# Delta rule, phase one: the keys' chain over more steps, gates' projections and the inversion spread anew

## The chip, the cores and the metric

One core of a Trainium2 chip runs the whole decoder trunk in one launch. The metric is the device time of one execution in microseconds (us); smaller is better. Engines named here: TensorE (PE in the rows, with PEld for its weight loads and "matmul" for what it runs), VectorE (DVE), ScalarE (ACT), GpSimd (POOL) and SyncE (SP), whose queue issues all the DMAs spoken of here.

## What is computed

Four residual layers of 1024 tokens x 1024 features: a gated convolution, forgetting attention, the gated delta rule, and sliding-window attention. The change lies in the third, the delta rule (8 heads of 128, chunks of the sequence). Its heart, cut from the reference (`k_beta` is k times beta):

```python
    L = jnp.where(strict, jnp.einsum('bhnid,bhnjd->bhnij', k_beta, k) * decay, 0.0)
    T = lax.linalg.triangular_solve(eye + L, jnp.broadcast_to(eye, L.shape), left_side=True, lower=True, unit_diagonal=True)
    u = T @ v_beta
    w = T @ (k_beta * jnp.exp(g_cum)[..., None])
    ...
    def step(state, xs):
        qd, kd, u_c, w_c, qk_c, gl = xs
        v_new = u_c - w_c @ state
        o = qd @ state + qk_c @ v_new
        state = state * jnp.exp(gl)[..., None, None] + jnp.einsum('bhck,bhcv->bhkv', kd, v_new)
        return state, o
    ...
    return (o * jax.nn.silu(z)) @ w_out
```

k comes from a projection, a causal convolution of four taps, SiLU and a normalisation; z is a projection too, and silu(z) is what the kernel calls a gate.

## The kernel before

Everything is laid out as 128 features x 512 tokens, two halves h of the sequence. Projections run in split float32: each chunk of 128 input features is three 512-column matmuls (high x high, high x low, low x high; L159 to L161), eight chunks for one output tile, and `proj_steps` yields after each. Weights are loaded raw and split in two parts, a ScalarE cast (hi) and a GpSimd subtraction (lo; `split_w`, L142 and L143; for gates `zsplit`, L1675 and L1676, tiles cv and QK).

Phase one of `layer_gdn` prepares the keys of 8 heads x 2 halves, numbered n = 0 to 15, and computes the gates beside them. `step(n)` for n = 1 to 17 strings pieces of generators together: `cur` is `keys(n)` (from step 16 on it is gates, then the later `fill`), `stage(m)` advances the keys started in step m by one yield, `zfill` advances the gates by one chunk, `dec` and `decs` the decay tile E, `g.advance(0, r)` the inversion by r yields. TensorE runs in the order in which this is written all through the phase, ScalarE and GpSimd do in steps 1 to 15; the order of VectorE and of SyncE is chosen by the framework's planner.

One key's pieces by yield, which the steps below name by number:

- 1 to 8: chunks of its projection (TensorE); 9: cb and cu from PSUM (ScalarE, L1297 and L1305), three conv instructions (VectorE, L1307)
- 10: tanh (ScalarE, L1313) and the last product, which gives kT (VectorE, L1314); 11: kT is stored by DMA
- 12: four transposes of kT (TensorE, L1322), four squares with sums (ScalarE, L1330), rk (VectorE, L1361), a power (GpSimd, L1362), kq (VectorE, L1364)
- 13: kd, four scalings (ScalarE, L1369), its store, kg and E x rk (GpSimd, L1371 and L1374), the store of E
- 14: a small transpose of kq (TensorE, L1379), its copy to a row (ScalarE, L1381) and the row's store gbr; 15: the load that spreads that row, br (L1385)
- 16: br x E (GpSimd, L1387); 17: four matmuls pa of kT with itself (TensorE, L1392), LT = pa x br (VectorE, L1394), its store gLT; 18: the load of the diagonal blocks into U (L1412, `blocks`)

In the kernel before, key n takes yields 1 to 10 in step n; 11 and 12 after five chunks of step n+1, 13 after the rest of its chunks, 14 at its end; 15 at the start of step n+2, 16 in the middle, 17 at its end; 18 at the start of step n+3.

`solve` inverts the 32 x 32 diagonal blocks of heads 0 to 3 (b = 0), row by row: for row i a product over i x i elements (split in two from row 23 on, L1428) and a reduction (L1431), all on VectorE, 71 yields and a last one that stores T twice (L1433, L1435, with a copy between). It needs U of keys 0 to 7. Steps 10 to 15 advance it by 6, 3 and 3 yields each. After step 15 `loads(0, 0)` brings T back as the tiles T1 and TT (L1461, L1459); `merge` (L1477 and on) uses them from the eleventh piece of step 17's `fill` on, and then the scan over chunks begins. Tiles have fixed buffers: E (TT) 3, kT 3, LT 3 (shared with a gate's raw weights), br (qT) 2, PSUM of pa 2.

Of the kernel before, what the change touches and what calls it, by code (L numbers as in the profile page):

```python
# [1186 lines left out]
class Gdn:  # L1187
# [226 lines left out]
    def solve(self, b, U):  # L1414
        p, nc = self.p, self.nc
        T = p.tile([P, 32, 32], F32, name="sT")
        nc.vector.memset(T, 0.0)
        nc.vector.memset(T.rearrange("p a b -> p (a b)")[:, 0:1024:33], 1.0)
        pr = p.tile([P, HT], F32, name="sp")
        for i in range(1, 32):  # L1420
            step = HT // i
            for n0 in range(0, i, step):
                n1 = min(i, n0 + step)
                n = n1 - n0

                m = i - n0
                v = pr[:, :n * m].rearrange("p (n j) -> p n j", j=m)
                nc.vector.tensor_tensor(v, T[:, n0:i, n0:n1].rearrange("p j n -> p n j"),  # L1428
                                        U[:, n0:i, i].unsqueeze(1).broadcast_to([P, n, m]), op=ALU.mult)
                yield  # L1430
                nc.vector.tensor_reduce(T[:, i, n0:n1], v, axis=AX.X, op=ALU.add, negate=True)  # L1431
            yield
        nc.sync.dma_start(out=self.T_d[b][0], in_=T)  # L1433
        nc.vector.tensor_copy(U, T.rearrange("p i n -> p n i"))
        nc.sync.dma_start(out=self.T_d[b][1], in_=U)  # L1435
        yield
# [211 lines left out]

FILL = 1300
HOPS = 13  # L1650
ZF = 5
LAG = 5

MORE = (25, 0, -25)
# [2 lines left out]
def layer_gdn(k, out):  # L1657
    with k.tc.tile_pool(name="gd", bufs=1) as p:
        g = Gdn(k, p)
# [21 lines left out]
        def gate(c, h):  # L1681
            load = h and c < 7
            if load:
                raws.append(zraw(c + 1, 1))
            for i, u in enumerate(k.gate2_steps(zs[c], c, h)):
                if i == 0 and not h and 0 < c < 7:
                    raws.append(zraw(c + 1, 0))
                if load and i % 4 == 3:
                    zsplit(c + 1, raws.pop(0))
                yield u  # L1690
# [11 lines left out]
        def take(it, n=1):  # L1702
            for _ in range(n):
                next(it, None)
# [3 lines left out]
        def stage(n, count=1):  # L1708
            take(stages.get(n, none), count)

        with k.tc.manual_schedule(engines={E_.PE}):
            other = k.gate2_steps(zs[0], 0, 1)
            for _ in range(8):
                take(half, 1)
                take(other, 1)
            take(half, 1)
            take(other, 1)
            gts = g.gates()
            take(gts, 17)
            zfill = itertools.chain(gate(1, 1), *(gate(c, h) for c in range(2, 8) for h in range(NH)))  # L1720
            g.wload(1, 0)
            fill = itertools.chain(*(g.prepare(i // 2, i % 2) for i in range(16)),
                                   itertools.islice(out, 6), g.values(), out)
            stages[0] = g.keys(0, 0, g.w[1])
            stage(0, 5)
            take(gts)
            stage(0, 4)
            take(zfill, ZF + 5)
            take(gts)
            take(zfill, 3)  # L1730
            take(gts)
            stage(0)
            late = g.decay(0, 0)
            take(late)

            def step(n):
                hd, h = n // 2, n % 2
                dec = decs.pop(0)
                if n < 16:
                    cur = stages[n] = g.keys(hd, h, g.w[1])  # L1740
                else:
                    cur = zfill if n == 16 else fill
                stage(n - 2)
                stage(n - 3)
                if n < 15 and h:
                    wraw = kraw.pop(0)
                    g.w[1] = [k.split_w(r, P) for r in wraw]
                if n > 1:
                    take(dec)
                if 10 <= n < 16:  # L1750
                    g.advance(0, 6)
                take(cur, 5)
                stage(n - 1, 2)
                take(cur, 4 if n < 16 else 3)
                if n == 1:
                    take(late, 2)
                    take(dec)
                stage(n - 1)
                stage(n - 2)
                if n < 14 and not h:  # L1760
                    kraw.append([k.raw_wk(g.w_in[j * 512:(j + 1) * 512, 1024 + (hd + 1) * P:1024 + (hd + 2) * P], P) for j in range(2)])
                if 10 <= n < 16:
                    g.advance(0, 3)
                take(zfill if n < 17 else fill, ZF)
                take(dec)
                if n < 16:
                    take(cur)
                decs.append(g.decay((n + 1) // 2, (n + 1) % 2) if n < 15 else none)
                take(decs[0])
                stage(n - 2)  # L1770
                stage(n - 1)
                if 10 <= n < 16:
                    g.advance(0, 3)
                if n == 14:
                    g.wload(0, 0)
                if n == 15:
                    g.wload(2, 0)

            decs = [g.decay(0, 1)]
            take(decs[0])  # L1780
            kraw = [[k.raw_wk(g.w_in[j * 512:(j + 1) * 512, 1024 + P:1024 + 2 * P], P) for j in range(2)]]
            with k.tc.manual_schedule(engines={E_.Activation, E_.Pool}):
                for n in range(1, 16):
                    step(n)
            g.ahead.append(g.loads(0, 0))
            for j in range(2):
                g.kd_load(j)
            step(16)
            step(17)
            stage(15)  # L1790
            take(zfill, 30)
            g.advance(1, 24)
            done = 0
            for i in range(16):
                while len(g.prep.get((i // 2, i % 2), ())) < 6:
                    next(fill)
                for j, extra in enumerate(g.scan(i // 2, i % 2)):
                    if i == 14 and j < 7:
                        k.split_y(j, 0)
                    quota = FILL // HOPS + (extra or 0)  # L1800
                    while done < quota:
                        c = next(fill)
                        done += c
                        if c == 0:

                            assert i == 15 and j > 3
                    done -= quota
            for _ in range(3):
                next(out)
            run(g.tail())  # L1810
            with k.tc.issue_after(k.mark.ins):
                for c in range(7):
                    k.split_y(c, 1)
# [72 lines left out]
```

## Time and profile before

| | |
|---|---|
| time, median of 3 runs | 2153.03 us (2152.46 to 2154.45) |
| profiled execution, its own time | 2149.09 us |
| its span, first to last instruction | 2147.4 us |
| TensorE busy | 2078.8 us, 97% |
| VectorE, ScalarE, GpSimd busy | 1323.6 us, 992.1 us, 836.8 us |
| mean granted TensorE clock | 0.992 |
| chain that ended last | TensorE 74%, VectorE 13%, ScalarE 4%, DMA 4% |

The profiled execution is one run: its span and 1.7 us around it are its time, and it lies 3.9 us under the median of the three. Times in the rows are microseconds from the span's start. An engine's busy share is an average over the whole program; what matters for the change is the stretch of phase one, from about 1080 to 1290 us. The ends of matmuls are modelled and overlap, so distances between their starts are used.

### The profile page before, as it was taken

To read this page: it belongs to the slowest core of one execution; us is meant where nothing else is said; L and a number is where in the kernel's file an instruction comes from. 1 tells how busy PE (TensorE), PEld (TensorE's weight loads), DVE (VectorE), ACT (ScalarE), POOL (GpSimd) and SP (SyncE) were. 2 spreads that over 40 slices of the span, in tenths; PEclk is the share of its full clock that TensorE was granted. 3 is DMA by queue.
4 is the path that set the end of the run, shared out by engine and by line. 5 is a ranking of instruction groups with operands and counts; after the bars stand their busy time and mean duration, and the time that the engine had idled before them with its cause. 6 is when DMAs were issued, how large, how long until landed. Compare 5 with 4: busy or idle time off the path is not lost.

```text
span 2147.4 us, 33391 instructions
## 1 busy us (share of the span) xinstructions
PE 2078.8 (97%) x11717; PEld 1748.3 (81%) x11717; DVE 1323.6 (62%) x2748; ACT 992.1 (46%) x2483; POOL 836.8 (39%) x721
## 2 busy tenths in 40 slices
PE   7999999999999999999999789999999999999998
PEld 5887888788898989888688677878888888878888
DVE  7657655544535355475455967775565568888874
ACT  6333334433433233454366443434443446666764
POOL 2244544731221221236356552322324545445630
PEclk9999999999999999999999999999999999999999
DMA  7122213741222321236256553342325521121134
GB/s 237 50 69 84 64 59 119 224 95 41 47 38 44 40 51 31 58 95 187 75 159 195 157 171 96 87 122 78 102 80 164 168 66 49 46 54 50 45 89 148
DMA packets 288366, 205.70 MB, mean 96 GB/s; under 512 B 41381, under 2 KB 245574, under 8 KB 288198
## 3 DMA queue, kind: packets, MB, share of 16 engines
q1 hardware_dynamic: 288198, 203.56, 33.9%
q8 instruction: 93, 1.52, 0.3%
q14 instruction: 75, 0.61, 0.1%
HBM read 154.87 MB, written 43.38 MB: 92 GB/s over the span
## 4 chain that ended last, share of the span: by engine, by line
PE 74%; DVE 13%; ACT 4%; DMA 4%; issue 3%; POOL 1%; SPq 0%; ACTq 0%; POOLq 0%; DVEq 0%
PE ps_pj L159 15%; PE ps_pj L160 15%; PE ps_pj L161 15%; PE ps_sc L248 2%; PE ps_sc L250 2%; PE ps_sc L249 2%; PE ps_pj L248 1%; PE ps_pj L249 1%; PE ps_pj L250 1%; PE ps_tr L835 1%; DVE sp L1428 1%; DVE cu L1307 1%; DVE lg L1153 1%; PE ps_pj L743 1%; PE ps_pj L745 1%
## 5 line engine op out<-in xcount | busy, mean ns | idle before, releaser
L159 PE MATMUL ps_pj<-hhi,whi 128*128 128x512 f32 (+1 forms) x1712 | 698.8, 409 | 3.5 <-ACT hhi L411 1.4
L160 PE MATMUL ps_pj<-hlo,whi 128*128 128x512 f32 (+1 forms) x1712 | 669.2, 391 | 7.2 <-DVE hlo L416 3.9
L161 PE MATMUL ps_pj<-hhi,wlo 128*128 128x512 f32 (+1 forms) x1712 | 669.0, 391 | 0.0
L143 POOL TENSOR_TENSOR wlo<-wraw,whi 128x512 fp32r<-128x512 f32 x296 | 404.4, 1373 | 615.9 <-ACT whi L142 584.9
L161 PEld LDWEIGHTS ps_pj<-hhi,wlo 128*128 128x128 f32 x1712 | 321.8, 188 | 68.9
L160 PEld LDWEIGHTS ps_pj<-hlo,whi 128*128 128x128 f32 x1712 | 323.3, 189 | 61.6 <-DVE hlo L416 5.1
L159 PEld LDWEIGHTS ps_pj<-hhi,whi 128*128 128x128 f32 x1712 | 323.1, 189 | 59.7 <-issue 2.5
L142 ACT CAST whi<-wraw 128x512 fp32r<-128x512 f32 x304 | 185.9, 617 | 312.1 <-PE ps_pj L160 172.7
L1307 DVE SCALAR_TENSOR_TENSOR cu<-cb,taps,cu 128x512 f32<-128x512 f32 x144 | 135.7, 942 | 12.3 <-ACT cu L1305 10.5
L1159 POOL TENSOR_TENSOR lg<-lg,st 128x512 f32<-128x512 f32 (+1 forms) x64 | 63.7, 996 | 122.7 <-DVE st L1158 117.3
L888 ACT ACTIVATE lg<-lg,mx 128x512 f32<-128x512 f32 (+2 forms) x96 | 58.7, 613 | 64.0 <-DVE mx L883 63.6
L1156 ACT ACTIVATE lg<-lg,st 128x257 f32<-128x257 f32 (+1 forms) x128 | 63.1, 494 | 49.2 <-DVE st L1153 49.0
L840 ACT CAST phi<-ps_tr 128x512 fp32r<-128x512 f32 (+1 forms) x80 | 40.6, 544 | 94.3 <-PE ps_tr L835 94.2
L461 DVE TENSOR_TENSOR y<-ps_pj,xr 128x512 f32<-128x512 f32 x56 | 38.5, 687 | 64.0 <-PE ps_pj L161 57.5
L841 DVE TENSOR_TENSOR plo<-ps_tr,phi 128x512 fp32r<-128x512 f32 (+1 forms) x80 | 49.5, 633 | 42.5 <-ACT phi L840 42.5
L469 DVE TENSOR_TENSOR acc<-acc,hf 128x512 f32<-128x512 f32 x49 | 48.5, 990 | 41.2 <-ACT hf L468 41.2
L143 POOL TENSOR_TENSOR wlo<-wr,whi 128x512 fp32r<-128x512 f32 x36 | 48.0, 1333 | 59.0 <-ACT whi L142 54.7
L1428 DVE TENSOR_TENSOR sp<-sT,sU 128x504 f32<-128x504 f32 (+18 forms) x80 | 57.0, 713 | 6.3 <-DMA sU<-gLT 5.1
L1153 DVE CUSTOM_DVE_ANT_0 lg<-ps_sc,band,sk 128x256 f32<-128x256 f32 (+1 forms) x128 | 55.0, 464 | 5.0 <-PE ps_sc L1148 3.4
L291 DVE SCALAR_TENSOR_TENSOR y<-y,ps_pj 128x512 f32<-128x512 f32 x48 | 32.7, 681 | 38.6 <-ACT y L290 38.6
L743 PE MATMUL ps_pj<-whi,hhi 128*128 128x256 f32 x192 | 54.8, 285 | 0.0
L744 PE MATMUL ps_pj<-wlo,hhi 128*128 128x256 f32 x192 | 54.6, 285 | 0.0
(448 smaller groups left out, 4613.5 us busy)
## 6 DMA issues: line engine op xcount, KB each, us to landing
xd<-y SPq DMA_DIRECT2D x64, 256.0 KB, 3.4
wraw<-in_fox_w_in_dram SPq DMA_DIRECT2D x60, 256.0 KB, 4.2
xr<-xd SPq DMA_DIRECT2D x56, 256.0 KB, 2.8
wraw<-in_gdn_w_in_dram SPq DMA_DIRECT2D x52, 256.0 KB, 3.7
wraw<-in_conv_w_in_dram SPq DMA_DIRECT2D x40, 256.0 KB, 3.0
wraw<-in_swa_w_in_dram SPq DMA_DIRECT2D x40, 256.0 KB, 2.9
wraw<-in_conv_w_out_dram SPq DMA_DIRECT2D x32, 256.0 KB, 4.9
wraw<-in_fox_w_out_dram SPq DMA_DIRECT2D x32, 256.0 KB, 2.8
```

The lines of the kernel that those rows point to most:

```text
L142: nc.scalar.copy(hi[:, :, :cols], raw[:, :, :cols])
L143: (eng or nc.gpsimd).tensor_tensor(lo[:, :, :cols], raw[:, :, :cols], hi[:, :, :cols].bitcast(F32), op=ALU.subtract)
L159: nc.tensor.matmul(o, hi, xhi, start=(c == 0), stop=False)
L160: nc.tensor.matmul(o, hi, xlo, start=False, stop=False)
L161: nc.tensor.matmul(o, lo, xhi, start=False, stop=(c == NC_ - 1))
L248: nc.tensor.matmul(ps, whi[:, c, :], xhi, start=start and c == 0, stop=False, skip_group_check=True)
L249: nc.tensor.matmul(ps, whi[:, c, :], xlo, start=False, stop=False, skip_group_check=True)
L250: nc.tensor.matmul(ps, wlo[:, c, :], xhi, start=False, stop=stop and c == 3, skip_group_check=True)
L743: nc.tensor.matmul(ps, xhi, whi, start=(c == 0), stop=False)
L1153: nc.vector.tensor_tensor_reduce(lg[:, u, :n], ps[:, u, :n], band[:, 2 * P - n:], 1.0, sk[:, hd:hd + 1], ALU.add, ALU.min, st[:, 0, u:u + 1])
L1307: eng.scalar_tensor_tensor(u, cb[:, j:j + HT], tap(j), u, op0=ALU.mult, op1=ALU.add)
L1428: nc.vector.tensor_tensor(v, T[:, n0:i, n0:n1].rearrange("p j n -> p n j"), U[:, n0:i, i].unsqueeze(1).broadcast_to([P, n, m]), op=ALU.mult)
```

## The change

Three numbers and the order inside `step` change; no instruction is added or taken away.

- A step takes 3 gate chunks (ZF) in steps 1 to 9 and 8 (ZL, four in the middle and four later) in steps 10 to 16, where it took 5 in each.
- The keys' pieces come later: 11 and 12 after all chunks of step n+1 and behind its conv, 13 at its end; 14 after two chunks of step n+2, 15 after five, 16 at its end; 17 at the start of step n+3, 18 in the middle.
- The inversion is advanced by the numbers of ROWS, three pieces in each of steps 10 to 15 (12, 12, 12, 10, 10 and 9 yields) and what is left in step 16; the first piece stands after five chunks. Step 16 is therefore issued ahead of `loads(0, 0)` and the first loads of kd.

```diff
--- before.py
+++ after.py
@@ -1648,7 +1648,10 @@
 
 FILL = 1300
 HOPS = 13
-ZF = 5
+
+ZF, ZL = 3, 8
+
+ROWS = {10: (4, 4, 4), 11: (4, 4, 4), 12: (4, 4, 4), 13: (4, 3, 3), 14: (4, 3, 3), 15: (3, 3, 3), 16: (99,)}
 LAG = 5
 
 MORE = (25, 0, -25)
@@ -1725,7 +1728,7 @@
             stage(0, 5)
             take(gts)
             stage(0, 4)
-            take(zfill, ZF + 5)
+            take(zfill, 10)
             take(gts)
             take(zfill, 3)
             take(gts)
@@ -1740,37 +1743,39 @@
                     cur = stages[n] = g.keys(hd, h, g.w[1])
                 else:
                     cur = zfill if n == 16 else fill
-                stage(n - 2)
+                rows = list(ROWS.get(n, ()))
+                solve = lambda: rows and g.advance(0, rows.pop(0))
                 stage(n - 3)
                 if n < 15 and h:
                     wraw = kraw.pop(0)
                     g.w[1] = [k.split_w(r, P) for r in wraw]
                 if n > 1:
                     take(dec)
-                if 10 <= n < 16:
-                    g.advance(0, 6)
-                take(cur, 5)
-                stage(n - 1, 2)
+                take(cur, 2)
+                stage(n - 2)
+                take(cur, 3)
+                stage(n - 2)
+                stage(n - 3)
+                solve()
+                if n in ROWS:
+                    take(zfill, ZL // 2)
                 take(cur, 4 if n < 16 else 3)
                 if n == 1:
                     take(late, 2)
                     take(dec)
-                stage(n - 1)
-                stage(n - 2)
+                stage(n - 1, 2)
                 if n < 14 and not h:
                     kraw.append([k.raw_wk(g.w_in[j * 512:(j + 1) * 512, 1024 + (hd + 1) * P:1024 + (hd + 2) * P], P) for j in range(2)])
-                if 10 <= n < 16:
-                    g.advance(0, 3)
-                take(zfill if n < 17 else fill, ZF)
+                solve()
+                take(zfill if n < 17 else fill, ZF if n < 10 else ZL - ZL // 2 if n < 17 else 5)
                 take(dec)
                 if n < 16:
                     take(cur)
+                stage(n - 2)
+                stage(n - 1)
                 decs.append(g.decay((n + 1) // 2, (n + 1) % 2) if n < 15 else none)
                 take(decs[0])
-                stage(n - 2)
-                stage(n - 1)
-                if 10 <= n < 16:
-                    g.advance(0, 3)
+                solve()
                 if n == 14:
                     g.wload(0, 0)
                 if n == 15:
@@ -1782,12 +1787,12 @@
             with k.tc.manual_schedule(engines={E_.Activation, E_.Pool}):
                 for n in range(1, 16):
                     step(n)
+            step(16)
             g.ahead.append(g.loads(0, 0))
             for j in range(2):
                 g.kd_load(j)
-            step(16)
             step(17)
-            stage(15)
+            stage(15, 2)
             take(zfill, 30)
             g.advance(1, 24)
             done = 0
```

## Rows read from the trace of the kernel before

**Rows 1.** The page: busy time, share of the span, instructions.

```profile
PE 2078.8 (97%) x11717; PEld 1748.3 (81%) x11717; DVE 1323.6 (62%) x2748; ACT 992.1 (46%) x2483; POOL 836.8 (39%) x721
```

**Rows 2.** Windows: length, busy time (instructions) by engine, clock, DMA share, GB/s.

```profile
1090.25:1173.89 83.64, 83.64 (x417) 69.50 (x417) 47.50 (x65) 55.20 (x179) 56.30 (x61) 1.00 0.66 197
1173.89:1260.96 87.07, 68.78 (x313) 55.16 (x312) 77.08 (x132) 43.32 (x137) 54.71 (x50) 0.94 0.57 161
```

**Rows 3.** What TensorE waited for, 1173.89 to 1260.96 (us, times, longest).

```profile
PE ps_tr L1322 <- DVE kT L1314: 15.0, 5, 5.2
PE ps_pj L161 <- POOL QK L1676: 2.7, 1, 2.7
PE ps_pj L159 <- ACT cv L1675: 0.6, 1, 0.6
```

**Rows 4.** Timeline of TensorE, step 8 and the first merge (start, length, instruction).

```profile
1152.99 0.60 PE L1322 MATMUL ps_tr<-ident,kT 128*128 128x128 f32 x4
...
1155.51 0.39 PE L159 MATMUL ps_pj<-hhi,cv 128*128 128x512 f32 x1
...
1159.00 1.05 PE L1392 MATMUL ps_sc<-kT 128*128 128x128 f32 x8
1159.89 0.27 PE L1379 MATMUL ps_ov<-ident,kq 128*4 128x128 f32 x1
...
1274.91 0.59 PE L1477 MATMUL ps_pj<-T,LT 32*32 32x32 f32 x16
```

**Rows 5.** Groups of VectorE's instructions, 1178 to 1251 (busy us, mean ns, idle before).

```profile
L1428 DVE TENSOR_TENSOR sp<-sT,sU 128x1 f32<-128x1 f32 (+29 forms) x40 | 32.3, 807 | 5.9 <-DMA sU<-gLT 5.1
L1431 DVE TENSOR_REDUCE sT<-sp 128x1 f32<-128x1 f32 (+30 forms) x40 | 15.5, 387 | 0.8
L1307 DVE SCALAR_TENSOR_TENSOR cu<-cb,taps,cu 128x512 f32<-128x512 f32 x15 | 14.9, 995 | 0.0
L1314 DVE SCALAR_TENSOR_TENSOR kT<-kT,cu 128x512 f32<-128x512 f32 x5 | 4.5, 895 | 0.0
```

**Rows 6.** Timeline of VectorE and GpSimd in the inversion.

```profile
1203.43 0.80 DVE L1428 TENSOR_TENSOR sp<-sT,sU 128x361 f32<-128x361 f32 x1
...
1216.76 2.78 POOL L143 TENSOR_TENSOR wlo<-wraw,whi 128x512 fp32r<-128x512 f32 x2 [1.96 <-ACT whi L142]
...
1217.06 1.24 DVE L1428 TENSOR_TENSOR sp<-sT,sU 128x1 f32<-128x1 f32 x1
```

**Rows 7.** Timeline of ScalarE, step 8: squares (first, last), cb, cu.

```profile
1153.68 0.28 ACT L1330 ACTIVATE jk<-ps_tr 128x128 f32<-128x128 f32 x1 [3.34 <-PE ps_tr L1322]
...
1155.06 0.19 ACT L1330 ACTIVATION_READ_ACCUMULATOR jk<-ps_tr 128x1 f32 x1
1155.71 0.59 ACT L1297 COPY cb<-ps_pj 128x512 f32<-128x512 f32 x1 [0.45 <-PE ps_pj L161]
1156.19 0.69 ACT L1305 ACTIVATE cu<-ps_pj,taps 128x512 f32<-128x512 f32 x1
```

**Rows 8.** Timeline of VectorE, step 8: rk and kq.

```profile
1155.29 0.24 DVE L1361 TENSOR_SCALAR rk<-rk 128x4 f32<-128x4 f32 x1 [3.27 <-ACT jk L1330]
1156.66 0.18 DVE L1364 TENSOR_TENSOR kq<-cols,rk 128x16 f32<-128x16 f32 x1 [1.13 <-POOL rk L1362]
```

**Rows 9.** What ScalarE waited for: 1173.89 to 1260.96, then 1090.25 to 1173.89.

```profile
ACT vb L1369 <- DVE kq L1364: 11.3, 5, 3.0
...
ACT vb L1369 <- DVE kq L1364: 0.4, 1, 0.4
```

**Rows 10.** Timeline of SyncE's queue: the row gbr and br of one key.

```profile
1151.62 0.35 SPq L1382 DMA_DIRECT2D gbr<-sn  x1
...
1155.09 0.33 SPq L1385 DMA_DIRECT2D qT<-gbr  x1
```

**Rows 11.** The inversion's last reduction (VectorE) and the first TT load (SyncE's queue).

```profile
1249.35 0.39 DVE L1431 TENSOR_REDUCE sT<-sp 128x15 f32<-128x225 f32 x1
...
1258.16 1.92 SPq L1459 DMA_DIRECT2D TT<-gT  x4
```

## Prediction

> **What bounds the kernel now.** I read the page first: TensorE is busy 97% of the span [rows 1], so only a stretch in which it is not fed can give much. The windows show the stretch: the eight steps before the inversion take 83.64 us with TensorE busy all the time, and the six steps with the inversion (10 to 15) take 87.07 us with TensorE busy 68.78 us, VectorE busy 77.08 us, and TensorE's granted clock at a mean of 0.94 against 1.00 [rows 2]. Eight steps in 83.64 us are 10.455 us for one; six at that pace would be 62.7 us, so the stretch loses 24.3 us. The waits say to whom: 15.0 us in five waits of the keys' transposes (L1322) for the final kT on VectorE, and 3.3 us for the split weights of a gate (QK, cv) [rows 3]. That is 18.3 us; the other 6.0 us are the half clock after the longer waits and the restarts. So 24.3 us (1.1% of the profiled execution's 2149.1 us) is the most that this change can win.
>
> **Prices on TensorE.** From one key's transposes to the next pa matmuls (L1392) lie 6.01 us: transposes and eight chunks. From pa to the small kq transpose (L1379, "pb" below) it is 0.89 us [rows 4]. With 10.455 us for a step of 13 chunks this gives 0.70 us for a chunk (three 512-column matmuls), 0.4 for the transposes, 0.9 for pa and pb.
>
> **Gates' chunks moved.** Steps 1 to 9 take 3 gate chunks for 5, steps 10 to 15 take 8 for 5, step 16 takes 16 in all for 13, and the three that were left over after step 17 are gone. Nothing is added: 18 + 3 chunks move. If TensorE is never starved, steps 1 to 9 take 10.455 - 1.4 = 9.06 us, steps 10 to 15 take 10.455 + 2.1 = 12.56 us, and all 24.3 us are won. Each wait of TensorE that is left or new is taken off that. The gates' other work (tanh, y, casts, QK, raw loads) moves along and is under a tenth of any engine's step.
>
> **The inversion over seven steps.** Its 80 VectorE instructions take 32.3 + 15.5 us [rows 5]. VectorE's 77.08 us plus some 4 us of step 16 (y, LT, rk, kq of the last keys) now lie beside 7 x 12.56 = 88 us of TensorE: it fits as a sum, where before 77 stood against 63. By steps it is uneven: step 13 (4, 3, 3) gets the ten instructions from the 361-element product to the single-element one; before, these and the keys' work among them took 14.9 us, from the first row to the end of the last, 1203.43 to 1218.30 [rows 6], of which some 5 us are the keys' (three conv instructions at 0.995, kT 0.9 [rows 5], LT, a y). In the new step 13 the same 14.9 us stand against 12.56. Steps 14 and 15 hold fewer instructions of the same sizes and come out near 13. So VectorE runs 2 to 3 us behind there. kT has room for it: its transposes now stand behind all eight chunks of the next keys and four gate chunks, 12.56 us after its own chunks, against some 6.5 us that the chain needs undisturbed (cb and cu 1.4 [rows 7], conv 3.0 and kT 0.9 [rows 5], a tanh and the handovers). So the 15.0 us of kT waits go; I keep none.
>
> **The keys' chain, moved.** This is where a new wait can come. Call t8 the end of a step's eighth chunk. Before, key n's transposes stood in mid step and pb followed 6.9 us after they began [rows 4]. Now the order is transposes at t8, 3 gate chunks (4 from step 10), pa, 2 chunks, pb: 0.4 + 2.1 + 0.9 + 1.4 = 4.8 us after t8 (5.5 from step 10). And ScalarE, whose order is also written out, now does cb and cu of the next conv before the squares. In step 8, t8 is at 1155.51, cb starts 0.20 later, cu ends at t8 + 1.37 [rows 4, 7]; four squares take 1.57 us [rows 7], so they end at t8 + 2.95; rk, the power on GpSimd and kq take from 1155.29 to 1156.84, 1.55 us [rows 8]. kq is ready at t8 + 4.6 with the handover: 0.2 us before TensorE comes to pb. But VectorE now has three conv instructions of 0.995 us from t8 + 1.45 on, just where rk and kq want it. If rk slips in after the second, pb stands 0.2 to 0.3 us late; behind the third, 1.3 us. VectorE's order is the planner's and not in the diff, so both ends stay. I take 0.5 us for each of steps 1 to 9: **4.5 us** (0 to 11.7).
>
> In steps 10 to 15 the arrival is at 5.5, and kq waits in a fuller queue. The nearest row: ScalarE's kd, which waits for kq, lost 11.3 us in these six steps, 1.9 each, against 0.4 us in the eight before [rows 9]. With that delay kq is ready at t8 + 6.5, and at 6.9 if a conv instruction is in its way too: a stall of 1.0 to 1.4 us. I take 0.3 in steps 10 to 12, where the inversion's rows are short, 1.4 in 13 to 15, 0.5 in step 16. In step 10 U comes later too: pa of key 7 moves from the end of step 9 to the start of step 10, and blocks behind it, so the first product (which had VectorE waiting 5.1 us for U before [rows 5]) waits in VectorE's queue in front of conv and rk: 1.5 us. Sum 0.9 + 4.2 + 0.5 + 1.5 = **7.1 us** (0 to 27).
>
> **SyncE and GpSimd.** E of key n+1 is loaded into the buffer that key n-2 leaves with br x E (L1387), and that multiply moves to the end of the step, so the load then reaches into the next step. br itself takes 3.5 us from its row's write to its load [rows 10] and has half a step more. GpSimd is busy 56.30 us in eight steps, 7.0 each [rows 2]; in a 9.06 us step that leaves 2 us of waiting, which I count as covered in the 0.5 above (its power sits in that chain).
>
> **The end of the inversion.** Before, the last reduction began at 1249.35 and the first TT load was issued at 1258.16, 9 us later, with T1's loads in between [rows 11]; the first merge came at 1274.91 [rows 4], 16.7 us after that. Now rows 30 and 31 (eight instructions, 4.8 us at the means of [rows 5]) and the copy are issued in step 16, VectorE has them done near its end, and the loads are issued behind step 16. The first merge comes 8 us into step 17 (pa, pb, ten chunks), its TT half two chunks later. The same 9 us from the inversion's end, and the loads' landing, meet it within a few us: **2.0 us** of wait (0 to 5). The cover of 16.7 us is spent.
>
> **Sum.** 24.3 - 4.5 - 7.1 - 2.0 = 10.7 us. Against the profiled execution 2149.1 - 10.7 = 2138.4; that execution lies 3.9 us under the median of 2153.0, so the median after is **2142.3 us** (0.5% faster).
>
> **Rivals.** *A, all covered:* rk and kq find gaps between the conv instructions, as they do in the undisturbed steps before (0.4 us lost in eight [rows 9]). Against it: there the squares came ahead of cb and cu. Only the merge costs: 2153.0 - 24.3 + 2.0 = 2130.7 us. *B, kq becomes the chain (slower):* rk always lands behind the third conv instruction, 1.3 us in steps 1 to 9 (11.7 us), and in steps 10 to 16 that 1.5, the 1.9 of [rows 9], and a GpSimd pass held against a VectorE product, 1.3, come to 4.7 - 0.9 of slack = 3.8 us in seven steps (26.6 us): 2153.0 - 24.3 + 38.3 + 2.0 = 2169 us. It decides from a mean pb wait of 24.3 / 16 = 1.5 us on; the 1.9 of [rows 9] speaks for it, the fact that a stalled TensorE gives VectorE time to catch up against it. That passes do hold each other shows in one row: a one-element product took 1.24 us, beginning 0.3 us after a GpSimd subtraction began, where the 361-element one took 0.80 [rows 6]. The Trainium skill, page "SBUF — State Buffer", section "Who interferes with whom", says that VectorE and GpSimd share one port pair under an exclusive lock, so that the later one is blocked until the other's instruction ends; this row agrees. By that rule the power and the third conv instruction would exclude each other in every step, some 0.75 us of stall for my 0.5, and the sum would be 2 us smaller. *C, no step gets shorter:* GpSimd's round (br, E, power, weights) holds steps 1 to 9 at 10.455, or T comes a whole step late at the merge; either takes about 10 us more: 2151 to 2153 us. *D:* the chunks move as the diff says in any case, since TensorE's order is written out; only VectorE's and SyncE's order is free.
>
> **How the numbers follow.** Forecast (2136 to 2149) 0.49, A 0.22, C 0.18, B 0.11. A change under 0.2% (4.3 us) can't be told from none here. Faster (under 2148.7): A, nearly all of the forecast and a bit of C, 0.74; same 0.18; slower 0.08 (most of B). The range from 2130 to 2153 leaves out the best of A and nearly all of B.
>
> **What would show it.** Right: steps 1 to 9 between 9.1 and 10.0 us from pa to pa; kT waits of L1322 gone or under 3 us; a new wait of L1379 (or its weight load) for kq; granted clock near 1.00 throughout. Wrong: kT waits still of 2 us and more in steps 12 to 15 (then VectorE's load was underrated); no wait for kq (A); kq waits over 1.5 us in most steps (B); a wait of L1477 or L1482 for T over 5 us (C).

## The result and the profile after

The changed kernel takes **2162.58 us** (median of 9 runs, 2156.98 to 2172.18) where the kernel before took 2152.71 us beside it: a ratio of 1.0052, 95% interval 1.0033 to 1.0070. The forecast was 2142.3 us, 0.5% faster; it is 0.5% slower, outside the range. The profiled execution took 2157.02 us, 5.6 us under its median, so the trace shows somewhat less than the runs do.

The page's first part (as [rows 1]) hides it, since TensorE is busy 97% as before. The windows tell more (columns as in [rows 2]; both rows from key 1's transposes to key 9's, and on to key 15's):

```profile
PE 2079.7 (97%) x11717; PEld 1746.6 (81%) x11717; DVE 1306.4 (61%) x2748; ACT 990.4 (46%) x2483; POOL 837.1 (39%) x721
```

```profile
1092.77:1183.44 90.67, 79.47 (x381) 63.91 (x380) 38.38 (x64) 52.47 (x176) 55.09 (x60) 0.96 0.62 181
1183.44:1272.94 89.50, 80.59 (x367) 64.70 (x366) 74.87 (x135) 45.34 (x142) 55.95 (x51) 0.94 0.54 157
```

At the prediction's pace the first row's eight steps hold 8 x 9.06 us and four of step 10's gate chunks, 75.3 us; they took 90.67. The second row's six steps hold 75.4 us and took 89.50. So the change loses 15.4 + 14.1 = 29.5 us where the kernel before lost 0 + 24.3. The six steps are better by 10 us; eight steps that had never lost anything lose 15. The first merge begins at 1287.80 (1274.91 in [rows 4]), 12.9 us later, and the span ends 7.6 us later.

What TensorE waited for in phase one, 1060 to 1300 (us, times, longest; as [rows 3]):

```profile
PE ps_ov L1379 <- DVE kq L1364: 21.2, 14, 3.3
PE ps_ov L1379 <- DVE cb L1299: 1.9, 1, 1.9
PE ps_pj L1493 <- ACT TT L1488: 0.5, 1, 0.5
PE ps_ov L1379 <- DVE sp L1428: 0.4, 1, 0.4
```

The 15.0 us of kT waits are gone, all of them, and so are the waits for gate weights. In their place stands pb (L1379), the small transpose of kq: 23.5 us in 16 waits, 1.47 us each. That is just below the 24.3 / 16 = 1.52 us from which the prediction's rival B decides.

**Why kq is late in the first eight steps.** What follows key 2's transposes, in order of time (steps 3 to 4, rows of several engines, picked out):

```profile
1105.58 0.19 ACT L1330 ACTIVATION_READ_ACCUMULATOR jk<-ps_tr 128x1 f32 x1
1105.88 0.16 DVE L1361 TENSOR_SCALAR rk<-rk 128x4 f32<-128x4 f32 x1
...
1106.00 0.75 DVE L1307 SCALAR_TENSOR_TENSOR cu<-cb,taps,cu 128x512 f32<-128x512 f32 x1
1106.13 1.49 POOL L1362 TENSOR_TENSOR rk<-rk,mhalf 128x4 f32<-128x4 f32 x1 [2.46 <-DVE rk L1361]
...
1107.60 1.26 POOL L1679 TENSOR_TENSOR QK<-os,cv 128x512 fp32r<-128x512 f32 x1
1107.65 1.23 DVE L1364 TENSOR_TENSOR kq<-cols,rk 128x16 f32<-128x16 f32 x1 [0.90 <-POOL rk L1362]
...
1109.03 0.27 PE L1379 MATMUL ps_ov<-ident,kq 128*4 128x128 f32 x1 [1.13 <-DVE kq L1364]
```

rk slipped in between two conv instructions, 0.1 us after the last square; that was not the trouble. The power, 1.01 us in its shortest case and in the median before the change, took 1.49 with a conv instruction beside it. Then kq, a product of 128x16 elements, took 1.23 us: it began 0.05 us after a GpSimd subtraction and ended with it. Before the change the same instruction took 0.18 us [rows 8]. All sixteen, before and then after (line by line: shortest, median, longest in ns):

```profile
L1364 DVE TENSOR_TENSOR kq<-cols,rk x16: 164/175/1222, 1084.2 to 1264.9; 128x16 f32<-128x16 f32 x16
```

```profile
L1364 DVE TENSOR_TENSOR kq<-cols,rk x16: 172/1227/1254, 1088.3 to 1279.6; 128x16 f32<-128x16 f32 x16
```

So the change itself made kq seven times as long, in ten of the sixteen cases. Before, GpSimd's written order had behind the power a copy of three columns (0.19 us) and then kg, which had to wait for kq:

```profile
1155.61 1.01 POOL L1362 TENSOR_TENSOR rk<-rk,mhalf 128x4 f32<-128x4 f32 x1
1156.58 0.19 POOL L1301 COPY halo<-cb 128x3 f32<-128x3 f32 x1
1156.90 0.19 POOL L1371 COPY kg<-kq 128x4 f32<-128x4 f32 x1
```

Now a subtraction or br x E stands there. In the ten long cases it was ready and began 0.05 to 0.25 us before kq; for keys 4, 5 and 6 br x E still waited for its DMA, and kq took 0.17 to 0.18 us. Key 13 does not fit so simply: its kq took 0.17 us inside a br x E that had begun 1.06 us before it and took 2.38. The Trainium skill, page "SBUF — State Buffer", section "Who interferes with whom", says that a VectorE instruction with two SBUF inputs contends with a GpSimd instruction that reads SBUF, that the shared port pair is an exclusive lock, and that issue order decides who blocks; the ten long cases agree.

**One step**, from key 6's transposes in step 7 to key 7's, took 13.20 us for 9.06. GpSimd and VectorE there:

```profile
1141.45 1.29 POOL L1387 TENSOR_TENSOR qT<-qT,TT 128x512 f32<-128x512 f32 x1 [2.82 <-DMA qT<-gbr]
1142.68 0.19 POOL L1371 COPY kg<-kq 128x4 f32<-128x4 f32 x1
1142.82 1.04 POOL L1374 TENSOR_TENSOR TT<-TT,rk 128x512 f32<-128x512 f32 x1
1143.82 2.54 POOL L143 TENSOR_TENSOR wlo<-wraw,whi 128x512 fp32r<-128x512 f32 x2
1146.34 0.64 POOL L1342 TENSOR_SCALAR_AFFINE_SELECT TT<-TT 128x512 f32<-128x512 f32 x1
1146.92 0.19 POOL L1303 COPY cb<-halo 128x3 f32<-128x3 f32 x1
```

```profile
1147.14 1.54 DVE L1307 SCALAR_TENSOR_TENSOR cu<-cb,taps,cu 128x512 f32<-128x512 f32 x2 [3.67 <-POOL cb L1303]
```

br x E waited 2.82 us for its DMA, six GpSimd instructions stood behind it, and the last, a copy of three columns into cb, kept VectorE's conv instructions, and rk behind them, waiting 3.67 us. pb of key 6 then waited 2.41 us, though kq took only 0.17. Two steps later the same copy held VectorE longer, and pb of key 8 waited 3.02 us:

```profile
1171.09 0.75 DVE L1307 SCALAR_TENSOR_TENSOR cu<-cb,taps,cu 128x512 f32<-128x512 f32 x1 [5.37 <-POOL cb L1303]
```

**The inversion was not spread.** Windows from its first product to behind its last reduction, and on to key 15's transposes:

```profile
1183.59:1251.20 67.61, 59.31 (x271) 47.86 (x269) 63.66 (x118) 32.54 (x106) 37.50 (x34) 0.92 0.46 130
1251.20:1272.94 21.74, 21.13 (x98) 16.69 (x97) 11.21 (x18) 12.80 (x36) 18.45 (x18) 1.00 0.78 242
```

VectorE is busy 63.66 of 67.61 us, 94%, and then 11.21 of 21.74. The last reduction ends at 1250.8, before at 1249.7 [rows 11]. The eight last instructions are written in step 16, behind key 14's transposes; they ran before them:

```profile
1246.83 0.60 PE L1322 MATMUL ps_tr<-ident,kT 128*128 128x128 f32 x4
...
1259.82 0.60 PE L1322 MATMUL ps_tr<-ident,kT 128*128 128x128 f32 x4
```

```profile
1243.32 1.10 DVE L1428 TENSOR_TENSOR sp<-sT,sU 128x510 f32<-128x510 f32 x1
...
1250.43 0.38 DVE L1431 TENSOR_REDUCE sT<-sp 128x15 f32<-128x225 f32 x1
```

So the planner, which orders VectorE, set rows ahead of where they are written. And in their queue stand rk and kq. For the pb of step 12 the last square ended at 1199.43; VectorE came to rk 3.2 us later, with rows of the inversion ahead of it and between:

```profile
1202.58 0.16 DVE L1361 TENSOR_SCALAR rk<-rk 128x4 f32<-128x4 f32 x1
1202.65 0.64 DVE L1428 TENSOR_TENSOR sp<-sT,sU 128x289 f32<-128x289 f32 x1
...
1204.24 1.19 DVE L1364 TENSOR_TENSOR kq<-cols,rk 128x16 f32<-128x16 f32 x1
```

**The clock charges again.** After the longer waits of pb the granted clock is at its lower level. Windows behind the 2.41 us wait, key 6's:

```profile
1151.00:1154.30 3.30, 3.30 (x9) 2.59 (x8) 0.15 (x1) 0.84 (x4) 0.99 (x1) 0.51 0.59 198
1154.30:1157.70 3.40, 3.40 (x18) 2.80 (x18) 0.69 (x1) 1.07 (x3) 1.43 (x3) 1.00 0.56 138
```

Nine matmuls at 0.51 in 3.3 us, then eighteen at 1.00 in 3.4: some 1.7 us lost each time. Phase one has six such stretches (one each behind the waits of 2.41, 3.02, 3.32 and 1.91 us, two in a row behind that of 3.01), before three.

### The profile page after: what moved, and what is told of

The parts are those of the page before. It is cut to its first block, busy times and chain, and to the rows that moved or that the text cites. A ratio compares the mean times of both kernels' runs of the same rounds, so it can differ in the third digit from the quotient of the medians.

```text
span 2155.0 us, 33402 instructions
## 1 busy us (share of the span) xinstructions
PE 2079.7 (97%) x11717; PEld 1746.6 (81%) x11717; DVE 1306.4 (61%) x2748; ACT 990.4 (46%) x2483; POOL 837.1 (39%) x721
## 3 DMA queue, kind: packets, MB, share of 16 engines
q8 instruction: 93, 1.52, 0.3%
## 5 line engine op out<-in xcount | busy, mean ns | idle before, releaser
L1307 DVE SCALAR_TENSOR_TENSOR cu<-cb,taps,cu 128x512 f32<-128x512 f32 x144 | 117.7, 817 | 52.4 <-ACT cu L1305 37.6
L1297 ACT COPY cb<-ps_pj 128x512 f32<-128x512 f32 x48 | 28.1, 584 | 96.2 <-PE ps_pj L161 96.2
L1428 DVE TENSOR_TENSOR sp<-sT,sU 128x504 f32<-128x504 f32 (+18 forms) x80 | 51.5, 644 | 7.1 <-DMA sU<-gLT 5.8
```

The source lines that it names most:

```text
L1307: eng.scalar_tensor_tensor(u, cb[:, j:j + HT], tap(j), u, op0=ALU.mult, op1=ALU.add)
```

## The experiments

Theory after these rows: the gates' move took cover away from a chain that the change had tightened; kq is late through the port and through VectorE's queue. "Lost" is the time over TensorE's pace from key 1's to key 9's and from there to key 15's transposes, worked out as above; kq is its median of 16 in ns. The kernel before lost 0 and 24.3, with 175. "Us" is a median; the kernel before, beside them, took 2150.5 to 2152.9 us, so runs are compared by the ratio. "Lost" and kq are of the one profiled execution, which lay up to 6.6 us (e18) from its kernel's median: 5.6 us below it for the change and e16, 6.0 above it for e7. Differences of a few us in "lost" are therefore weaker than the ratios.

| run | us | ratio (95%) | lost | kq |
|---|---|---|---|---|
| the change | 2162.6 | 1.0052 (1.0033 to 1.0070) | 15.4 + 14.1 | 1227 |
| e4 chain alone | 2148.5 | 0.9988 (0.9977 to 0.9999) | 3.9 + 17.2 | 1092 |
| e16 chain, gates | 2164.7 | 1.0062 (1.0048 to 1.0077) | 15.5 + 14.8 | 1228 |
| e17 chain, rows | 2148.1 | 0.9980 (0.9969 to 0.9991) | 3.3 + 17.0 | 1018 |
| e3 gates, rows | 2158.6 | 1.0038 (1.0026 to 1.0051) | 7.8 + 16.1 | 176 |
| e6 kg first | 2157.7 | 1.0030 (1.0018 to 1.0042) | 9.9 + 15.8 | 174 |
| e1 pb later | 2155.3 | 1.0023 (1.0011 to 1.0035) | 10.9 + 15.3 | 1230 |
| e2 squares first | 2163.8 | 1.0058 (1.0036 to 1.0080) | 16.4 + 19.1 | 176 |
| e5 fourth E | 2162.3 | 1.0041 (1.0025 to 1.0056) | 11.6 + 17.8 | 1232 |
| e7 = e1, e5, e6 | 2150.8 | 0.9993 (0.9979 to 1.0007) | 4.1 + 17.5 | 175 |
| e8 = e4, e6, e1 | 2156.3 | 1.0020 (1.0010 to 1.0030) | 3.8 + 25.6 | 174 |
| e9 rows pinned | 2157.4 | 1.0024 (1.0010 to 1.0037) | 13.0 + 12.9 | 1230 |
| e10 = e7, pinned | 2150.8 | 0.9993 (0.9980 to 1.0006) | 5.5 + 11.6 | 176 |
| e11 = e4, pinned | 2152.8 | 1.0004 (0.9986 to 1.0021) | 3.5 + 17.6 | 1232 |
| e12 kq on GpSimd | 2160.4 | 1.0037 (1.0023 to 1.0051) | 13.3 + 11.6 | 216 |
| e14 = e10, e12 | 2147.2 | 0.9975 (0.9965 to 0.9984) | 5.8 + 7.0 | 216 |
| e15 before, kq on GpSimd | 2150.4 | 0.9994 (0.9982 to 1.0005) | 0.7 + 23.0 | 215 |
| e13 = e4, e12 | 2143.3 | 0.9955 (0.9941 to 0.9968) | 1.7 + 20.5 | 216 |
| e18 = e17, e12 | 2146.9 | 0.9966 (0.9956 to 0.9977) | 1.1 + 18.3 | 217 |

The theory that a run was to test missed its range of time in e1, e2, e3, e5, e7, e8, e9, e10, e12 and e18, and by 0.1 us in e6; e16 lay 0.7 us above the range for a loss through the gates' move. e4, e13, e14, e15 and e17 came out in the range that the theory gave. e11, expected at 2143 to 2147 us if rows set ahead make kq late, shows no gain from pinned rows on the chain alone; e8 is told below.

**Which part loses.** e4, e16 and e17 are the changed kernel with one or two of its parts undone:

```diff
# e4: gates as before, rows in steps 10 to 15 alone, loads ahead of step 16
-ROWS = {10: (4, 4, 4), ..., 13: (4, 3, 3), 14: (4, 3, 3), 15: (3, 3, 3), 16: (99,)}
+ROWS = {n: (4, 4, 4) for n in range(10, 16)}
-take(zfill if n < 17 else fill, ZF if n < 10 else ZL - ZL // 2 if n < 17 else 5)
+take(zfill if n < 17 else fill, ZF)        # ZF = 5; none in mid step
# e16: e4 with the change's gates; e17: e4 with the change's ROWS and order of loads
```

> The changed kernel with only the keys' chain in its new order: 5 gate chunks in every step and the inversion in six steps of 12 yields. Theory K: TensorE comes to pb 6.2 us after the eighth chunk, kq is ready at about 6.1 in steps 1 to 9, so waits there are under 0.5 us each, but in steps 10 to 15, with VectorE full, 2 us and more each; kT waits are gone; in all no faster than before, 2148 to 2160 us. Rival V: the stretched chain alone takes the kT waits away, 2136 to 2142 us.

> The changed kernel without its spreading of the inversion: chain moved, gates' chunks moved, rows written in steps 10 to 15 at (4, 4, 4), loads of the first group ahead of step 16. Chain alone is 2148.5 us, the whole change 2162.6 us. If the gates' move carries the loss (steps 1 to 9 at 9.06 us run ahead of GpSimd's and ScalarE's round), 2159 to 2164 us. If the rows' spreading and the later loads carry it, 2147 to 2152 us.

> The changed kernel without its move of the gates: chain moved, rows written over seven steps and the first group's loads behind step 16. Since the planner sets the rows ahead of their steps anyway, theory H gives no difference to the chain alone, 2147 to 2151 us, with the last reduction within 2 us of 1255. If the loads behind step 16 make the inverse's blocks come late at the first merge, 2152 to 2156 us.

On this chain it is the gates' move, alone. e16 stands with the whole change, nearly step for step (first rows, from key 1's to key 9's transposes and on to key 15's); e4 (second rows) loses 9.2 us less in them, and its median is 16.2 us lower:

```profile
1091.93:1182.76 90.83, 79.58 (x382) 63.99 (x380) 38.40 (x64) 52.42 (x176) 54.69 (x60) 0.96 0.62 181
1182.76:1272.97 90.21, 80.61 (x368) 64.67 (x367) 75.22 (x135) 45.32 (x142) 55.44 (x51) 0.94 0.55 156
```

```profile
1093.92:1181.46 87.54, 84.01 (x418) 68.59 (x417) 40.90 (x65) 53.93 (x179) 57.99 (x61) 1.00 0.63 184
1181.46:1261.35 79.89, 68.09 (x313) 54.46 (x312) 72.53 (x132) 42.62 (x137) 53.00 (x48) 0.94 0.57 172
```

Taking 16 chunks (11.2 us) out of the first eight steps and putting four of step 10's in should shorten 87.54 to 79.1 us; they became 90.83. Putting 18 chunks (12.6 us) into the next six made them 10.3 us longer: 2.3 us of them were hidden. And e17 equals e4: spreading the rows and issuing loads later does nothing, as the rows run when U allows. The chain's move alone gains 0.1%, with an interval (0.9977 to 0.9999) that barely leaves out no gain.

> The kernel before with only the gates' chunks (3 in steps 1 to 9, 8 from step 10) and the inversion's seven steps of the change; the keys' chain stays as it was, pb at the end of the step. Theory K: no waits on L1379; the kT waits of 15 us fall to 3 to 8 us since four gate chunks more stand in front of the transposes; 2136 to 2148 us. Rival V (moving the gates and the inversion is what costs): 2155 us or more.

e3 is the kernel before with the change's ZF, ZL, ROWS and order of loads, and the keys' pieces where they were. It loses as well, without any stretched kq: in steps 2 to 8 kT waits of 0.6 to 1.2 us keep each step at 9.9 to 10.5 us, and 11.8 us of waits for kq come in steps 10 to 16. A step of 9.06 us was too short for the old chain too.

But what the gates' move costs hangs on the chain. With e6's and e1's edits (shown next) the chain without the gates' move, e8, was expected at 2138 to 2146 us and took 2156.3, against 2150.8 for e7, which has the gates' move (and e5's edit and the spread rows) besides. In e8 pb waits 1.1 us in all, and the transposes wait for kT again:

```profile
PE ps_tr L1322 <- DVE kT L1314: 15.9, 8, 4.0
```

**Why steps 2 to 9 don't shorten.** e6 puts kg, kd and E x rk right behind the power, so that GpSimd's next pass waits for kq; e1 puts pb behind all five chunks; e2 puts transposes and squares ahead of cb and cu; e5 gives E a fourth place, so that its load needn't wait for br x E.

```diff
# e6                          # e1                     # e5, in decay()
-stage(n - 1, 2)              -take(cur, 2)            -E = p.tile(..., name="TT", bufs=NB)
+stage(n - 1, 3)              -stage(n - 2)            +E = p.tile(..., name="sp") if hd * 2 + h in (3, 7)
 ...                          -take(cur, 3)            +    else p.tile(..., name="TT", bufs=NB)
-stage(n - 1)  # step's end   -stage(n - 2)
                              +take(cur, 5)
                              +stage(n - 2, 2)
# e2: transposes and squares before piece 9 (cb, cu)
-take(cur, 4 if n < 16 else 3)
+take(cur, 3); stage(n - 1, 2)
+if n < 16: take(cur)
-stage(n - 1, 2)
```

> The changed kernel with piece 13 (kd, kg, E x rk) issued right behind piece 12 instead of at the end of the step, so that GpSimd has kg, which waits for kq, behind the power, and no long two-input pass can begin between the power and kq. Theory K with the port: kq takes 0.17 us again where it took 1.23 us, waits on L1379 in steps 1 to 6 fall by 0.9 to 1.0 us each to under 0.3 us, the steps take 9.1 to 9.5 us; 5 to 10 us faster than the changed kernel. Theory R: GpSimd then waits for br or E instead, the steps stay at 10 us, and the time stays within 3 us of the changed kernel.

> The changed kernel with one move: piece 14 (the small transpose of kq, L1379) comes after five chunks of the step, together with 15, instead of after two. Theory K (kq is late for its transpose): TensorE comes to it 2.1 us later, 6.9 us after the eighth chunk's end in steps 1 to 9 and 7.6 after that, and kq was there at about 6.1; of 23.5 us of waits on L1379 at most 5 are left, the granted clock goes back to 1.00 in most of the stretch, and the time is 2130 to 2142 us. Rival V (the steps are too short for VectorE and GpSimd, whatever stands where): the wait only moves, to the kT transposes (L1322) or a gate's weights, and the time stays at 2155 us or more.

> The changed kernel with the other end of the chain moved: key n-1's transposes and squares are issued right after the eighth chunk but ahead of this step's conv, so ScalarE does the four squares before cb and cu. Theory K: kq is ready 1.2 us earlier for the missing cb and cu and some more because the three conv instructions no longer lie before rk, so waits on L1379 fall from 23.5 to under 6 us and the time is 2130 to 2144 us; the conv comes 1.6 us later, which kT's transposes, a step later, have room for. Rival V: 2155 us or more, with waits of L1322 for kT.

> The changed kernel; only the decay tiles E of keys 3 and 7 lie in the inversion's product tile (unused in steps 1 to 9), so E has four places instead of three there and its load no longer waits for br x E of three keys before. Theory R (a ring holds the short steps: br x E frees E's buffer, E's load waits for that at the head of SyncE's queue, the row gbr and the load of br stand behind it, and br x E of the next key waits for br): steps 3 to 8 lose their worst cases, the 13.2 us of step 7 falls under 11 us and GpSimd's waits for br to under 1 us each; about 4 to 8 us faster than the changed kernel, 2150 to 2156 us. Theory K alone (kq's own chain of squares, rk, power, kq): no change in steps 1 to 6, 10.0 us each; at most 1 us faster.

> The changed kernel with all three: E's fourth place, piece 13 behind 12, and piece 14 after five chunks. If kq's chain and the ring are the whole cause in steps 1 to 9, these take 9.1 to 9.5 us and the clock stays whole there; in steps 10 to 16 kq still waits behind the inversion's products, 1 us a step. 2138 to 2146 us, faster than both. If the short steps are bound by something else (VectorE and GpSimd excluding each other), steps 1 to 9 stay near 10 us: 2150 us or more.

e6 is the test of the port: kq is back at 159 to 176 ns in every step, the first eight steps lose 9.9 for 15.4 us, and the time falls by 4.9 us (by ratios of 1.0030 and 1.0052, whose intervals overlap).

```profile
L1364 DVE TENSOR_TENSOR kq<-cols,rk x16: 159/174/176, 1090.2 to 1274.8; 128x16 f32<-128x16 f32 x16
```

So what stands behind the power is shown as the cause of the long kq. The third of the first steps' loss that goes is that of the whole move, since kd and E x rk come earlier too; what kq's length alone costs is not shown. e1 gains most (6 to 7 us): three chunks later, pb gives kq 2.1 us more; 19.4 us of waits stay. e2 brings kq back to 176 ns but moves part of the wait to kT (9.5 us; pb still waits 12.3), and gains nothing. e5 brings nothing alone: the place of E is not what binds. Together (e7) steps of 9.08 to 9.18 us appear, TensorE's pace, between others of 9.9 to 10.6; the first eight lose only 4.1 us. But the six steps with the inversion then lose 17.5.

**Why the late steps don't fill.** e9 holds each call of the rows to its step:

```diff
-solve = lambda: rows and g.advance(0, rows.pop(0))
+def solve():
+    if rows:
+        with k.tc.issue_after(g.final.ins):    # the last kT written so far
+            g.advance(0, rows.pop(0))
```

> The changed kernel, and each call of the inversion's rows may only be issued behind the key projection's last step on VectorE that was written ahead of it (kT of L1314). In the changed kernel the planner set the rows written for step 14 at 1218.79 to 1229.46, two to three steps ahead of where they are written, so that the reductions ended at 1250.81 after 67 us in which VectorE was 94% busy, and rk and kq stood in its queue behind them. Theory H (the rows set ahead of their steps make kq late): with the rows held to their steps the last reduction falls into step 16, the 16.5 us of waits of the row product for kq in steps 9 to 15 go down to under 6 us, steps 10 to 15 shorten from 89.5 to 80 us or less, and the time falls by 6 to 10 us, to 2151 to 2156 us. Rival P (VectorE holds less than its queue, whatever the order, and the shared port makes rk and kq slow): the waits stay over 12 us and the time within 2 us of 2162.6. Rival T (the inverse comes late): the waits go, but the first merge begins after 1290 and the time is 2162 us or more.

> The kernel with the row product behind all five chunks, kg, kd and the decays' product right behind the power, and a fourth place for E (2150.8 us, ratio 0.9993), and the rows held to their steps as well. Its steps 10 to 15 took 93 us while steps 1 to 9 took 89; if the rows set ahead are what makes the late steps long, they come down to 80 to 84 us and the time to 2140 to 2145 us, faster than the kernel before by 0.3 to 0.6%. If VectorE's or the port's capacity is what binds there, the time stays at 2149 to 2153 us. If the inverse comes late, the merges wait and the time is 2153 us or more.

The rows do go to step 16 now (VectorE, and TensorE's transposes of key 15):

```profile
1272.82 1.68 DVE L1428 TENSOR_TENSOR sp<-sT,sU 128x496 f32<-128x496 f32 x1
...
1275.86 0.39 DVE L1431 TENSOR_REDUCE sT<-sp 128x15 f32<-128x225 f32 x1
```

```profile
1270.28 0.60 PE L1322 MATMUL ps_tr<-ident,kT 128*128 128x128 f32 x4
```

pb's waits stayed, 24.7 us in all for 23.5: in steps 9 to 15 they fell from 12.9 us (the expectation has 16.5) to 10.5, and in steps 16 and 17 they rose from 2.3 to 6.0. So neither theory is right alone: the time fell by 5.2 us, short of the theory's 6 to 10, while the waits did what its rival said. In e10 pinning does bring the loss of the six steps down, from 17.5 to 11.6 us, and it is given back: from key 15's transposes to the first merge 15.7 us pass for 11.2, with 2.65 us of pb's wait and 0.9 us of the merge's for T among them. The last reduction comes at 1270.1 for 1244.3, the first merge at 1278.1 for 1277.1, and the time is the same to a hundredth. That rows run ahead of their steps is shown; that they cost time is not.

**kq on GpSimd.** Sum rk and product kq move beside the power, so that neither stands in VectorE's queue nor shares the port:

```diff
-nc.vector.tensor_scalar(rk, rk, EPS, None, op0=ALU.add)
+nc.gpsimd.tensor_scalar(rk, rk, EPS, None, op0=ALU.add)
-nc.vector.tensor_tensor(kq, ...)
+nc.gpsimd.tensor_tensor(kq, ...)
```

> The changed kernel, with the sum rk (L1361) and the product kq (L1364) on GpSimd, around the power that is there already: neither stands in VectorE's queue any longer, and no other pass of GpSimd can take the shared port between the power and kq. Theory K (VectorE's queue and the port between power and kq make kq late): the row product's waits of 23.5 us go down to under 10 us and the time falls by 6 to 12 us, to 2150 to 2157 us. Rival G (GpSimd's own round holds kq: 131 of 240 us busy in phase one, so that sum and kq wait behind decay products and weights): the waits stay over 15 us and the time stays above 2159 us, or rises. Rival S (the squares themselves, on ScalarE, come late): the same waits, but the sum on GpSimd begins within 0.3 us of the last square.

> The chain's move alone (2148.5 us, ratio 0.9988), with sum rk and product kq on GpSimd. Theory K: its 10.1 us of waits for kq fall to under 4 us, the steps of 12 us (3 and 9) become 10.4, and the time falls by 3 to 8 us, to 2141 to 2146 us, faster than the kernel before by 0.3 to 0.5%. Rival G: 2148 us or more.

> The kernel with the three small moves and the rows held to their steps (2150.8 us), with sum rk and product kq on GpSimd as well. Its waits for kq were 5.6 us, for cv 6.4 and for kT 4.0 us. Theory K gives 2145 to 2149 us: about 4 us of the waits for kq go, and VectorE is rid of 16 products of 1.2 us in the stretch in which it is full. Rival G: GpSimd holds QK (L1679) longer and the waits for cv grow by as much, 2150 us or more.

> The kernel before, with sum rk and product kq on GpSimd, for comparison with the chain moved and the same edit (2143.3 us, ratio 0.9955). In the kernel before, the row product stands after kq by a whole half step and never waits for it; what the edit can bring there is only VectorE's time in the inversion (12 small operations, about 4 us) in a stretch where it is 97% busy. If the chain's move with kq cured is what gains, this kernel stays at 2149 to 2153 us. If the edit alone carries the gain, it comes to 2145 us or less.

> The changed kernel without its move of the gates (2148.1 us, ratio 0.9980), with sum rk and product kq on GpSimd. The chain alone fell from 2148.5 to 2143.3 us by that edit, with its waits for kq going from 10.1 to 1.4 us. Here the waits for kq are 9.2 us: if the two edits add up, 2141 to 2144 us, faster than the kernel before by 0.35 to 0.5%. If the 5 us came from elsewhere than the waits for kq, 2145 to 2149 us.

kq takes 216 ns in the median there. On the whole change (e12) pb's waits stay at 23.5 us all the same, now through GpSimd's own round, which the rival said:

```profile
1117.81 1.29 POOL L1387 TENSOR_TENSOR qT<-qT,TT 128x512 f32<-128x512 f32 x1 [3.33 <-DMA qT<-gbr]
...
1122.66 0.65 POOL L1342 TENSOR_SCALAR_AFFINE_SELECT TT<-TT 128x512 f32<-128x512 f32 x1 [2.43 <-DMA TT<-g_d]
...
1123.53 0.23 POOL L1361 TENSOR_SCALAR rk<-rk 128x4 f32<-128x4 f32 x1
1123.84 1.05 POOL L1362 TENSOR_TENSOR rk<-rk,mhalf 128x4 f32<-128x4 f32 x1
```

It waits for br, then for the load of E, and rk comes behind; pb waited 2.74 us at 1125. With the gates left where they were (e13), steps of 10.45 us leave room for that round, and the waits of pb all but vanish:

```profile
PE ps_tr L1322 <- DVE kT L1314: 9.3, 5, 2.6
PE ps_pj L161 <- POOL QK L1679: 4.0, 1, 4.0
PE ps_ov L1379 <- POOL kq L1364: 1.4, 2, 1.1
```

e13 (0.9955) and e18 (0.9966) beat both kernels; without the chain's move the same edit does nothing (e15). Where e13's 8.6 us lie is open: its profiled execution, the slowest of its five, has the first merge only 2.3 us earlier than the kernel before. e18 missed the 2141 to 2144 us that it would have taken if the two edits added up: its waits for kq fell from 9.2 to 1.3 us, and the ratio only from 0.9980 to 0.9966, with intervals that overlap. By the reading set down before it, e13's gain then comes from elsewhere than the waits for kq; but by the intervals e13 and e18 are not to be told apart either, so this stays open.

## Why the prediction was wrong, step by step

- **The bound and the prices** were right. A step of 3 gate chunks that nothing holds took 9.08 us for the predicted 9.06 (e7), one of 8 took 12.50 to 12.52 for 12.56 (e14's steps 10 to 12).
- **kT waits all go**: right (0 us). But for one of the two reasons only: the transposes stand later. VectorE got little relief: it was busy 94% of the inversion, before 97%.
- **"If TensorE is never starved"**: the move of the gates was costed as if 10.455 us of a step were TensorE's need alone. It was also about what the round of SyncE, GpSimd, ScalarE and VectorE took in the orders tried: e3, e16 and e12 hold the first eight steps at 10.0, 11.0 and 10.7 us in the mean by three different waits (kT on VectorE, kq on VectorE, kq on GpSimd), and the change took 11.0 for the predicted 9.06 + 0.5. Four of e7's seven steps from key 1's to key 8's transposes took 9.08 to 9.18, so what held them was the order of the chain and not the engines' busy time. This is the step that failed: taking the chunks out uncovered the round, and eight steps that had lost nothing lost 15.4 us. Rival C named it, as a thing that would cost what it hid; with stalls it cost more.
- **"The keys' chain, moved", 4.5 us for steps 1 to 9**: measured 9.7 us in steps 2 to 9. rk slipped in early, as taken; the missing pieces were the GpSimd pass behind the power (kq 1.23 us for 0.18), which I counted only in rival B and only from step 10 on, though [rows 6] showed it, and the power itself, 1.49 us for 1.01. The sentence that by the port's rule the sum would be 2 us smaller looked at the power and the conv instruction, and not at kq.
- **7.1 us for steps 10 to 16**: measured 13.8 us in steps 10 to 17 (3.0, 0.4, 3.3, 1.6, 3.0, 0.3, 0.3 and 1.9), inside the range of 0 to 27. But it did not come where the sum put it: steps 10 and 12 had 2.1 us and took 6.3, 3.0 of them before the inversion's first row (the copy into cb above) and 3.3 beside its rows 15 to 18. For steps 13 to 15 the sum took 4.2 us and 4.8 were measured, which is in part luck, since the rows there ran ahead of their steps.
- **"The inversion over seven steps"**: wrong. It took 67.6 us, 94% of VectorE, and in the chain alone 68.9 (e4: 1186.6 to 1255.5). I took VectorE's order, which the prediction itself called the planner's, for the written one. The ten instructions counted for step 13 are eleven (six products, five reductions); nothing hangs on it.
- **"SyncE and GpSimd ... covered"**: held in most steps and failed between key 6's transposes and key 7's, 13.20 us, and again two steps later, 16.51 us for 11.86 (15 chunks).
- **The merge, 2.0 us**: no wait of L1477 for T at all; the inverse was there early, since rows ran early.
- **A term was missing.** The 24.3 us held 6.0 us of clock and restarts beside the waits, but new waits were charged without any. With 23.5 us of waits and six stretches at 1.7 us the sum is 24.3 - 23.5 - 10.2 = -9.4 us, a loss; the scan's first matmul (L1591) begins at 1307.29, before at 1296.33, 11.0 us later, and the medians lie 9.9 us apart.
- **Rival B** gave 2169 us with the right wait, the right engine and the right break-even, and had 0.11. Its count of 38.3 us was too high (23.5), its clock term absent; that it lies only 6 us from the result is in part luck.

## What to carry to other kernels

A step that looks bound by TensorE may be about as long as the slowest round of the other engines; before taking filler out of it, add up the latency of that round (waits, DMAs and queues), not the busy times. When an instruction moves in one engine's written order, look at what now stands right behind its neighbours on the engine that shares a port: a ready pass there made a 0.18 us product 1.23 us long in ten of sixteen cases. And a new wait is charged with what the clock takes after it. When one late piece is cured, look where the wait goes: in e8 it went from kq to kT, and the kernel was slower than without the cure.

## What was not expected of the hardware

- A VectorE product of 128x16 elements took 175 ns in the median before the change and 1.19 to 1.25 us behind a GpSimd pass of 128x512 that had begun 0.05 to 0.25 us before it, in ten of the changed kernel's sixteen cases; the same product on GpSimd itself took 216 ns in the median (e12).
- GpSimd's power over 128x4 elements took from 1.01 to 2.54 us (median 1.49) in the changed kernel, with VectorE's conv instructions and rows beside it; before, 1.01 in the median.
